# Hybrid RG-LRU / retention block on one core: gelus of the gate branch in groups, exponentials and roots in blocks, and the softplus spread over the convolution

## The chip, the cores and the metric

The kernel runs on one core of one Trainium2 chip. The metric is the device time of one execution in microseconds. TensorE (PE in the profile) multiplies matrices, VectorE (DVE) and ScalarE (ACT) do elementwise work, SyncE (SP) starts the loads. Each engine takes its instructions in a fixed order; an instruction waits until what it reads is written and until the buffer that it writes is free. ScalarE's functions live in tables: a function that is not in the table at hand needs an ACT_TABLE_LOAD ahead of it, which the compiler puts in.

## What is computed

A transformer-like block on 528 tokens (16 meta tokens and 512 of input), width 1024. One wide projection feeds a recurrent branch, a gate, a retention branch and two output gates; a feed-forward part follows. The change concerns the recurrent branch and its gate:

```python
u_rnn, u_gate, q, k, v, g_ret, ga, gb = jnp.split(rms_norm(h, norm_mix_g) @ w_in, IN_SPLITS, axis=-1)
xr = causal_dwconv(u_rnn, rnn_conv_w, rnn_conv_b)
# rg_lru, in 10 blocks of 128 channels:
r = sigmoid(xr @ w_a + b_a);  i = sigmoid(xr @ w_x + b_x)
log_a = -8.0 * r * softplus(-lam)
a = exp(log_a);  b = sqrt(-expm1(2.0 * log_a)) * (i * xr)
h_t = a_t * h_(t-1) + b_t
o_a = hr * gelu(u_gate)
```

`q` and `k` then get a rotary embedding, and retention follows.

## The kernel before

The tokens lie along the free axis (528 columns, the last 514 of them for the gate and for q), 128 channels on the partitions. Weights arrive as fp32 (`raw`, three buffers of 1 MB each) and are split into a high and a low fp16 half (`wt`, ten buffers): `split` (L94, L95) takes the high half on ScalarE and the low half on VectorE. Three fp16 products stand for one fp32 product, so a projection of 128 channels is 48 matmuls. A new weight load may start when VectorE has done the splits of the unit that held its buffer; `tick()` puts one split into the program at a time.

The stages around the change, in program order:

- Ten convolution steps. Step n multiplies u_rnn's block n (`conv_product`), from step 3 on multiplies the two gates of block n-3 (`rnn_gates`: two groups of six matmuls, two sigmoids on ScalarE, L663, one product on VectorE, L665), and applies the four taps (`conv_taps`: one ScalarE instruction L645, three VectorE instructions L647). `conv_split` splits the result (`xs`).
- The softplus of lambda on a 128 x 10 tile (L710 to L727): one absolute value, one exponential, 24 small VectorE instructions, a series for the logarithm.
- Ten gate products (loop at L732). Each takes 48 matmuls, one split, a gelu straight out of PSUM (L737), and by a table (`SPREAD`) groups of five of the recurrent branch's steps: tanh (`rnn_tanh`, L668), exponential with two VectorE products (`rnn_decay`, L672, L674, L675), square root (`rnn_root`, L678), and the scan over tokens (`rnn_scan`, a product L682 and a scan L683). The gates of blocks 7, 8 and 9 fall into the first three of them.
- For each of four heads the projections of q and k with their rotary embedding (`rotary`): two products, then on VectorE for each of two halves a product with the cosines (L773), one with the sines (L774) and their sum (L775), and a split. The second L773 and the second L774 are the last readers of the two PSUM tiles. Between them stand the remaining scans and the gating of the branch (`branch_a`, product L750 and a split). Products take PSUM tiles from a pool of four, so a projection needs a tile that the rotary of the projection before last still reads.

Until the tenth gate product the order on TensorE, ScalarE and VectorE is that of the program (`manual_schedule`, closed by `order.close()` at L754); behind it a scheduler orders the instructions. In retention, `head_norm` takes a square root (L1057) and the gate units copy PSUM with L892.

Of the kernel before, what the change touches and what calls it, by code (L numbers as in the profile page):

```python
# [21 lines left out]
NR = DR // P  # L22
# [4 lines left out]
TQ = T - T0  # L27
# [5 lines left out]
SW = 2.0 ** 8  # L33
S_XN = 4.0
# [19 lines left out]
def hybrid_block_kernel(ctx, tc, x, meta, norm_mix_g, w_in, conv_w, conv_b, rg_a_w, rg_a_b,  # L54
                        rg_x_w, rg_x_b, lam, w_brnn, w_bret, w_out, norm_ffn_g, w_up,
                        fconv_w, fconv_b, w_down, norm_final_g, rope_t, decay_t, out):
    nc = tc.nc
    const = ctx.enter_context(tc.tile_pool(name="const", bufs=1))
# [17 lines left out]
    def acc(name):  # L76
        return psum["acc"].tile([P, 2, 512], F32, name=name, tag="acc")
# [115 lines left out]
    def unit_load(cuts=1):  # L193

        nk, ncol, parts, fast = units[len(loaded)]
        raw = wraw.tile([P, 2048], F32, name="raw")
        n = nk * ncol
        rv = raw[:, :n].rearrange("p (k c) -> p k c", k=nk)
        for k0, c0, ap in parts:
            load(rv[:, k0:k0 + ap.shape[1], c0:c0 + ap.shape[2]], ap)  # L200
        loaded.append(len(loaded))
        if fast:
            return fast_steps(rv, nk // 2, ncol // 2)
        hk = nk // 2
# [12 lines left out]
        return [step(i, c) for i in range(2) for c in range(cuts)]
# [74 lines left out]
    ahead = [6]  # L292
    current = [0]

    def unit_tiles(u):
        return 4 if units[u][3] else 2

    def emit_step():
        u, run = steps[done[0]]
        while len(loaded) < min(u + 3, len(units)):  # L300
            queue(unit_load())
        run()
        done[0] += 1

    def queue(new):
        steps.extend((len(loaded) - 1, run) for run in new)
# [9 lines left out]
    def tick(n=1, late=True):  # L316


        for _ in range(n):
            if done[0] == len(steps):  # L320
                if len(loaded) == len(units):
                    return
                queue(unit_load())
            u = steps[done[0]][0]
            if sum(unit_tiles(i) for i in range(current[0], u + 1)) > ahead[0]:
                return
            if gating[0] and not late and hasattr(steps[done[0]][1], "late"):
                return
            emit_step()
# [10 lines left out]
    vt1 = const.tile([P, P], F32, name="vt1")  # L340
# [72 lines left out]
    def x_of(hi, lo):  # L413
        tv = (hi, lo)
        return lambda a, k, c0, n: tv[a][:, k, c0:c0 + n]
# [7 lines left out]
    def run_of(ps, halves, j=0, n=None):  # L423
        c0 = 512 - halves[0][1] + j
        n = n or halves[0][1] + halves[1][1]
        return ps.rearrange("p a b -> p (a b)")[:, c0:c0 + n]

    def project(ps, w, col, src, halves, nk, turns=False):

        both = [0, 1]  # L430
        for hfs in [both] if turns else [[0], [1]]:
            for k, (aw, ax), hf in [(k, s, hf) for k in range(nk) for s in SPLIT for hf in hfs]:
                    c0, n = halves[hf]
                    nc.tensor.matmul(half_of(ps, halves, hf), w(aw, k, col, P), src(ax, k, c0, n),  # L434
                                     start=k == 0 and (aw, ax) == (0, 0), stop=k == nk - 1 and aw == 1)
# [6 lines left out]
    HQ = [(XF + T0, 256), (XF + T0 + 256, 258)]  # L442
# [167 lines left out]
    half_r, half_t, half_x, gate_g = {}, {}, {}, {}  # L610

    def part(hv, n):
        if n not in hv:
            hv[n] = piece([P, T], F32, "rnn")
        return hv[n]
# [27 lines left out]
    def conv_taps(n, ps):  # L643
        xv = part(half_x, n)
        nc.scalar.activation(xv, run_of(ps, HR, 3, T), AF.Identity, scale=cwr[:, 30 + n:31 + n], bias=b_conv[:, n:n + 1])  # L645
        for j in (2, 1, 0):
            nc.vector.scalar_tensor_tensor(xv, run_of(ps, HR, j, T), cwr[:, 10 * j + n:10 * j + n + 1], xv,  # L647
                                           op0=ALU.mult, op1=ALU.add)
# [6 lines left out]
    def rnn_gates(n):  # L655
        xs = xr_split.pop(n)
        xr = part(half_x, n)
        gi = wtile("gi")
        for nm, bias, dst in (("a", b_a, part(half_r, n)), ("x", b_x, gi)):
            ps = acc("ps")  # L660
            wt = gw[nm][0][n // 4]
            project(ps, lambda a, k, c0, m: wt[:, a, n % 4 * P:n % 4 * P + P], 0, x_of(xs[:, 0], xs[:, 1]), HG, 1)
            nc.scalar.activation(dst, run_of(ps, HG), AF.Sigmoid,  # L663
                                 scale=1.0 / (SW * S_XR), bias=bias[:, n:n + 1])
        nc.vector.tensor_mul(xr, xr, gi)  # L665

    def rnn_tanh(n):
        nc.scalar.activation(part(half_t, n), part(half_r, n), AF.Tanh, scale=cpos[:, n:n + 1])  # L668
# [11 lines left out]
    def rnn_scan(n):  # L680
        r, t, xr = part(half_r, n), part(half_t, n), part(half_x, n)
        nc.vector.tensor_mul(t, t, xr)  # L682
        nc.vector.tensor_tensor_scan(xr, r, t, 0.0, op0=ALU.mult, op1=ALU.add)  # L683

    LAG = 3
    load_gates("a")
    load_gates("x")
    queue(unit_load())
    for n in range(NR):
        ps = conv_product(n)  # L690
        if n == 0:
            split_gates("a")
        if n >= LAG:
            tick(2 if n in (4, 6, 8) else 1)
            rnn_gates(n - LAG)
        conv_taps(n, ps)
        if n == 0:
            conv_split(0)
        if n == 1:
            split_gates("x")  # L700
        if n == 2:
            tick()
            conv_split(1)
            psum_layout(acc=4)
        if n >= 2:
            conv_split(n)


    lv = vt1[:, 70:80]
    sp = const.tile([P, 8, NR], F32, name="sp")  # L710
    nc.vector.tensor_scalar(sp[:, 0], lv, -1.0, 0.0, op0=ALU.mult, op1=ALU.max)
    nc.scalar.activation(sp[:, 1], lv, AF.Abs)
    nc.scalar.activation(sp[:, 2], sp[:, 1], AF.Exp, scale=-1.0)
    nc.vector.tensor_scalar_add(sp[:, 3], sp[:, 2], 2.0)
    nc.vector.reciprocal(sp[:, 4], sp[:, 3])
    nc.vector.tensor_mul(sp[:, 4], sp[:, 4], sp[:, 2])
    nc.vector.tensor_mul(sp[:, 5], sp[:, 4], sp[:, 4])
    nc.vector.memset(sp[:, 6], 1.0 / 15.0)
    for m in (13, 11, 9, 7, 5, 3, 1):
        nc.vector.tensor_mul(sp[:, 6], sp[:, 6], sp[:, 5])  # L720
        nc.vector.tensor_scalar_add(sp[:, 6], sp[:, 6], 1.0 / m)
    nc.vector.tensor_mul(sp[:, 6], sp[:, 6], sp[:, 4])
    nc.vector.scalar_tensor_tensor(sp[:, 7], sp[:, 6], 2.0, sp[:, 0], op0=ALU.mult, op1=ALU.add)
    cneg = const.tile([P, NR], F32, name="cneg")
    cpos = const.tile([P, NR], F32, name="cpos")
    nc.vector.tensor_scalar_mul(cneg, sp[:, 7], -8.0)
    nc.vector.tensor_scalar_mul(cpos, sp[:, 7], 8.0)  # L727


    ahead[0] = 6  # L730
    SPREAD = ((rnn_tanh, 2, 0), (rnn_decay, 3, 0), (rnn_tanh, 4, 5), (rnn_decay, 5, 5), (rnn_root, 7, 0), (rnn_scan, 7, 0), (rnn_root, 9, 5))
    for n in range(NR):  # L732
        ps = acc("ps")
        u, col = u_ug[n // 2], (n % 2) * P
        project(ps, get(u), col, xf, HQ, KD)
        tick()
        nc.scalar.activation(part(gate_g, n)[:, :TQ], run_of(ps, HQ),  # L737
                             AF.Gelu_apprx_tanh, scale=1.0 / (SW * S_XN))
        if n < LAG:
            rnn_gates(NR - LAG + n)  # L740
        for f, n0, m0 in SPREAD:
            if n == n0:
                for i in range(m0, m0 + 5):
                    f(i)

    oa = {}

# [30 lines left out]
            split(dst[m][:, 0, :n], dst[m][:, 1, :n], turned[m][:, :n], s)  # L778

    def between(i):  # L780
        if i < 5:
            rnn_scan(5 + i)
        for n in ((i,), (5, 6), (7, 8), (9,))[max(0, i - 4)]:
            branch_a(n)

# [442 lines left out]
    for i in range(2):  # L1228
# [5 lines left out]
        ps = branch(u_ba, oa_of, NR)  # L1234
# [311 lines left out]
    for j in range(12):  # L1546
# [21 lines left out]
        else:  # L1568
# [4 lines left out]
            for m in range(2):  # L1573
                f = 2 * j + m
# [210 lines left out]
```

## Time and profile before

| | |
|---|---|
| time, median of 3 runs | 1058.54 us (1058.52 to 1058.54) |
| the profiled execution | 1058.55 us |
| its span, first to last instruction | 1056.8 us |
| TensorE busy | 1038.8 us |
| VectorE busy | 872.0 us |
| ScalarE busy | 594.3 us |
| granted TensorE clock | 0.999 of full speed |

The convolution steps run to about 86 us of the span, the gate products from 81 to 138 us on TensorE, the rotary projections from 138 to 225.5 us. A row of the timeline has the start, the time until the group's last end, engine, line, operation, output and inputs, shapes, and how many instructions it merges; in brackets stands the engine's idle time before it and what ended that. Engines overlap neighbouring instructions a little, so a row's duration is somewhat longer than the distance to the next start. A row of groups has busy time, the mean of one in ns, and the idle time before them. A row of waits has who waited for whom, the total, how often, and the longest. In a row of stretches stand, behind the two bounds and the length, the busy times of PE, PEld (weight loads), DVE, ACT and POOL, then the granted clock, DMA's share and GB/s.

### The profile page before, as it was taken

To read this page: it belongs to the slowest core of one execution; us is meant where nothing else is said; L and a number is where in the kernel's file an instruction comes from. 1 tells how busy PE (TensorE), PEld (TensorE's weight loads), DVE (VectorE), ACT (ScalarE), POOL (GpSimd) and SP (SyncE) were. 2 spreads that over 40 slices of the span, in tenths; PEclk is the share of its full clock that TensorE was granted. 3 is DMA by queue.
4 is the path that set the end of the run, shared out by engine and by line. 5 is a ranking of instruction groups with operands and counts; after the bars stand their busy time and mean duration, and the time that the engine had idled before them with its cause. 6 is when DMAs were issued, how large, how long until landed. Compare 5 with 4: busy or idle time off the path is not lost.

```text
span 1056.8 us, 21446 instructions
## 1 busy us (share of the span) xinstructions
PE 1038.8 (98%) x9187; PEld 866.2 (82%) x9187; DVE 872.0 (83%) x1327; ACT 594.3 (56%) x942; POOL 6.9 (1%) x20
## 2 busy tenths in 40 slices
PE   8999999999999999999999999999999999999997
PEld 6888888875588888888888886588888888888884
DVE  6885799989669999997797785479989898988965
ACT  7558973444356758666454453375555555454432
POOL 2000000000000000000000000000000000000000
PEclk9999999999999999999999999999999999999999
DMA  9241253331013132334333355032433324114312
GB/s 295 94 132 58 81 180 120 123 120 41 1 41 113 49 106 74 102 111 154 102 115 120 111 209 180 1 120 81 160 102 99 120 81 144 58 61 145 96 41 80
DMA packets 109311, 111.52 MB, mean 106 GB/s; under 512 B 5674, under 2 KB 101136, under 8 KB 109216
## 3 DMA queue, kind: packets, MB, share of 16 engines
q1 hardware_dynamic: 108640, 109.74, 32.5%
q8 instruction: 72, 1.18, 0.5%
q10 hardware_dynamic: 288, 0.27, 0.1%
q0 software_dynamic: 288, 0.14, 0.1%
q14 instruction: 23, 0.19, 0.1%
HBM read 108.04 MB, written 2.10 MB: 104 GB/s over the span
## 4 chain that ended last, share of the span: by engine, by line
PE 74%; DVE 15%; ACT 8%; issue 2%; DMA 0%; ACTq 0%; DVEq 0%
PE ps L434 27%; PE P L1603 10%; PE pa L886 9%; DVE wt L95 4%; PE pe L886 4%; PE ps L1320 4%; PE pm L434 3%; PE ps L448 3%; PE pb L886 2%; PE ps L950 2%; PE pa L1490 2%; ACT wt L94 2%; PE ps L1040 2%; PE pa L974 1%; DVE raw L262 1%
## 5 line engine op out<-in xcount | busy, mean ns | idle before, releaser
L434 PEld LDWEIGHTS <-wt 128*128 128x128 f16 x3840 | 372.8, 97 | 53.4 <-issue 1.3
L95 DVE SCALAR_TENSOR_TENSOR wt<-raw,wt 128x1024 f16<-128x1024 f32 (+2 forms) x286 | 310.4, 1102 | 54.0 <-ACT wt L94 52.9
L94 ACT ACTIVATE wt<-raw 128x1024 f16<-128x1024 f32 (+2 forms) x286 | 267.8, 958 | 117.8 <-PE P L1603 23.1
L886 PEld LDWEIGHTS <-wt 128*128 128x128 f16 x2016 | 195.3, 97 | 32.4 <-issue 5.7
L434 PE MATMUL ps<-x2h,wt 128*128 128x258 f16 (+1 forms) x1184 | 196.2, 273 | 0.0
L434 PE MATMUL ps<-xh,wt 128*128 128x258 f16 (+4 forms) x1056 | 177.5, 275 | 1.6 <-DVE t L773 1.6
L434 PE MATMUL ps<-x2l,wt 128*128 128x256 f16 (+1 forms) x592 | 161.0, 272 | 0.0
L434 PE MATMUL ps<-xl,wt 128*128 128x256 f16 (+4 forms) x528 | 140.8, 274 | 0.0
L1603 PE MATMUL P<-wt,act 128*128 128x256 f16 x792 | 88.3, 273 | 0.0
L1603 PEld LDWEIGHTS <-act 128*128 128x128 f16 x792 | 77.4, 98 | 9.0
L886 PE MATMUL pa<-xs,wt 128*128 128x258 f16 x576 | 71.3, 273 | 1.9 <-ACT kept L892 1.5
L1468 DVE SCALAR_TENSOR_TENSOR cv<-ps,vt,cv 128x512 f32<-128x512 f32 x80 | 59.5, 747 | 9.1 <-ACT cv L1466 8.5
L434 PE MATMUL pm<-oa,wt 128*128 128x256 f16 (+1 forms) x480 | 54.1, 273 | 0.0
L262 DVE TENSOR_TENSOR raw<-raw 128x1024 f32<-128x1024 f32 x43 | 52.5, 1220 | 0.7
L886 PE MATMUL pa<-ob,wt 128*128 128x257 f16 x384 | 45.7, 274 | 0.6 <-ACT last L892 0.5
L1320 PE MATMUL ps<-wt,mx 128*128 128x512 f16 x192 | 44.3, 379 | 0.0
L950 PE MATMUL ps<-wt,xh 128*128 128x512 f16 x128 | 38.3, 379 | 0.7 <-ACT qk L94 0.5
L1466 ACT ACTIVATE cv<-ps,vt,vt 128x512 f32<-128x512 f32 x40 | 30.5, 766 | 11.9 <-PE ps L434 11.9
L1490 PEld LDWEIGHTS <-wt 128*128 128x128 f16 x336 | 32.6, 97 | 4.4
L1320 PEld LDWEIGHTS <-mx 128*128 128x128 f16 x192 | 17.6, 98 | 18.5
L94 ACT ACTIVATE qk<-t 128x514 f16<-128x514 f32 (+1 forms) x16 | 10.2, 638 | 39.6 <-DVE t L775 39.6
L448 PEld LDWEIGHTS <-wt 128*128 128x128 f16 x288 | 27.9, 97 | 5.0 <-issue 0.5
(327 smaller groups left out, 1504.5 us busy)
## 6 DMA issues: line engine op xcount, KB each, us to landing
raw<-in_w_in SPq DMA_DIRECT2D x36, 1024.0 KB, 5.1
raw<-in_w_up SPq DMA_DIRECT2D x24, 1024.0 KB, 5.2
raw<-in_w_down SPq DMA_DIRECT2D x48, 256.0 KB, 3.7
raw<-in_w_branch_ret SPq DMA_DIRECT2D x16, 512.0 KB, 4.9
raw<-in_w_in SPq DMA_DIRECT2D x12, 512.0 KB, 4.8
raw<-in_w_branch_rnn SPq DMA_DIRECT2D x8, 640.0 KB, 4.7
raw<-in_w_out SPq DMA_DIRECT2D x4, 1024.0 KB, 5.1
xin<-in_x SPq DMA_DIRECT2D x4, 512.0 KB, 5.8
```

The costliest lines, as they stand in the source:

```text
L94: a = nc.scalar.activation(hi, src, AF.Copy, scale=s)
L95: b = nc.vector.scalar_tensor_tensor(lo, src, s, hi, op0=ALU.mult, op1=ALU.subtract)
L262: nc.vector.tensor_tensor(pair, pair, rv[:, :, right].rearrange("p (h k) c -> p h k c", h=2), op=ALU.add)
L434: nc.tensor.matmul(half_of(ps, halves, hf), w(aw, k, col, P), src(ax, k, c0, n), start=k == 0 and (aw, ax) == (0, 0), stop=k == nk - 1 and ...
L448: mm = nc.tensor.matmul(half_of(ps, halves, hf), w(aw, k, col, P), src(ax, k, c0, n), start=k == 0 and (aw, ax) == (0, 0), stop=k == KD - ...
L886: nc.tensor.matmul(ps[:, :n], ws[k // 4](wf, aw, k % 4), src(xf_, ax, k), start=first and k == 0 and (aw, ax) == (0, 0), stop=k == last_k ...
L950: nc.tensor.matmul(pb, xf(ax, k, XF + j0, nb), w(aw, k % 4, 0, 512), start=i == 0, stop=i == 23)
L1320: nc.tensor.matmul(ps[:, n], mx[k][:, a, c0:c0 + P], wo[k // 2](aw, k % 2, n * 512, 512), start=k == 0 and (a, aw) == (0, 0), stop=k == ks ...
L1466: nc.scalar.activation(vv_, taps[2], AF.Identity, scale=vt2[:, 96 + ch:97 + ch], bias=bias)
L1468: nc.vector.scalar_tensor_tensor(vv_, taps[j], vt2[:, 48 * j + ch:48 * j + ch + 1], vv_, op0=ALU.mult, op1=ALU.add)
L1490: nc.tensor.matmul(ps[:, :258], w(wf, aw, k), x2_form(xf_, ax, k), start=first and k == 0 and (aw, ax) == (0, 0), stop=k == 3 and aw == 1, ...
L1603: nc.tensor.matmul(pd[:, 256 * tt:256 * tt + 256], t[:, ax, c0 + tt * P:c0 + tt * P + P], w(wf, aw, i), start=q % 6 == 0 and tt == 0 and i ...
```

## The change

The softplus is cut in two. `softplus_exp` puts its first maximum, the absolute value and the exponential into convolution step 2. `softplus_rest` is a generator that gives out the VectorE instructions in five pieces, in steps 3 to 7, ahead of the split of the step; the series is written with fewer instructions (a product and an addition in one, no memset), so 16 are left. The tanhs of blocks 0 to 5 move into steps 8 and 9, between the taps and the split.

In the gate loop, all products but those of 5, 8 and 9 are copied out of PSUM with the scale (AF.Copy), and their gelus are done later in place: 0 to 4 ahead of 5's, 6 and 7 ahead of 8's. A product's gelu or copy now comes behind the recurrent steps that two tables, FIRST and THEN, place in its turn. Exponentials are done in turns 2, 3 and 4, roots in turns 6 and 7, eight of the ten scans in turns 7 to 9. The gates of blocks 8 and 9 are both put behind product 1.

```diff
+    def softplus_exp():
+        lv = vt1[:, 70:80]
+        nc.vector.tensor_scalar(sp[:, 0], lv, -1.0, 0.0, op0=ALU.mult, op1=ALU.max)
+        nc.scalar.activation(sp[:, 1], lv, AF.Abs)
+        nc.scalar.activation(sp[:, 2], sp[:, 1], AF.Exp, scale=-1.0)
+
+    def softplus_rest():
+        nc.vector.tensor_scalar_add(sp[:, 3], sp[:, 2], 2.0)
+        nc.vector.reciprocal(sp[:, 4], sp[:, 3])
+        nc.vector.tensor_mul(sp[:, 4], sp[:, 4], sp[:, 2])
+        yield
...
         conv_taps(n, ps)
+        if LAG <= n < 8:
+            next(series)
+        if n >= 8:
+            for i in range(3 * (n - 8), 3 * (n - 8) + 3):
+                rnn_tanh(i)
...
         if n == 2:
+            softplus_exp()
             tick()
...
-    SPREAD = ((rnn_tanh, 2, 0), (rnn_decay, 3, 0), (rnn_tanh, 4, 5), (rnn_decay, 5, 5), (rnn_root, 7, 0), (rnn_scan, 7, 0), (rnn_root, 9, 5))
+    FIRST = {0: (rnn_tanh, (6,)), 1: (rnn_tanh, (7,)), 2: (rnn_tanh, (8, 9)), 5: ("gelu", range(5)), 6: (rnn_root, range(5)), 7: (rnn_root, range(5, 10)),
+             8: ("gelu", (6, 7))}
...
+    def gate_gelu(i, src=None, s=1.0):
+        g = part(gate_g, i)[:, :TQ]
+        nc.scalar.activation(g, g if src is None else src, AF.Gelu_apprx_tanh, scale=s)
...
-        nc.scalar.activation(part(gate_g, n)[:, :TQ], run_of(ps, HQ),
-                             AF.Gelu_apprx_tanh, scale=1.0 / (SW * S_XN))
-        if n < LAG:
-            rnn_gates(NR - LAG + n)
...
+        if n in (5, 8, 9):
+            gate_gelu(n, run_of(ps, HQ), 1.0 / (SW * S_XN))
+        else:
+            nc.scalar.activation(part(gate_g, n)[:, :TQ], run_of(ps, HQ), AF.Copy, scale=1.0 / (SW * S_XN))
+        for i in ((7,), (8, 9))[n] if n < 2 else ():
+            rnn_gates(i)
...
     def between(i):
-        if i < 5:
-            rnn_scan(5 + i)
+        if i < 2:
+            rnn_scan(8 + i)
```

On ScalarE, this stands from the gelu or copy of gate product 3 on, before (L737 gelus, L672 exponentials, L668 tanhs, L94 weight splits):

```order
L737 ACT_TABLE_LOAD
L737 ACTIVATE rnn<-ps 128x514
L672 ACT_TABLE_LOAD
L672 ACTIVATE rnn<-rnn,cneg 128x528 x5
L94 ACTIVATE wt<-raw 128x1024
L737 ACT_TABLE_LOAD
L737 ACTIVATE rnn<-ps 128x514
L668 ACTIVATE rnn<-rnn,cpos 128x528 x5
L94 ACTIVATE wt<-raw 128x1024
```

and from the copy of product 3 on now (L767 copies, L753 gelus, L678 roots):

```order
L767 ACTIVATE rnn<-ps 128x514
L94 ACTIVATE wt<-raw 128x1024
L672 ACTIVATE rnn<-rnn,cneg 128x528 x4
L767 ACTIVATE rnn<-ps 128x514
L94 ACTIVATE wt<-raw 128x1024
L753 ACT_TABLE_LOAD
L753 ACTIVATE rnn<-rnn 128x514 x5
L753 ACTIVATE rnn<-ps 128x514
L94 ACTIVATE wt<-raw 128x1024
L678 ACT_TABLE_LOAD
L678 ACTIVATE rnn<-rnn 128x528 x5
L767 ACTIVATE rnn<-ps 128x514
```

The table loads between gelus and exponentials are gone there, and one load serves six gelus.

On VectorE, this stands around the rotary of head 0's q before (the scans L683 are printed as SCALAR_TENSOR_TENSOR; `t` is the rotary's tile, L773 to L775 its steps):

```order
L773 TENSOR_TENSOR t_1956<-ps,rope_1842 128x514
L683 SCALAR_TENSOR_TENSOR rnn<-rnn 128x528
L95 SCALAR_TENSOR_TENSOR wt<-raw,wt 128x1024
L682 TENSOR_TENSOR rnn<-rnn 128x528 x2
L683 SCALAR_TENSOR_TENSOR rnn<-rnn 128x528
L95 SCALAR_TENSOR_TENSOR wt<-raw,wt 128x1024 x2
L774 TENSOR_TENSOR t_1957<-ps,rope_1843 128x514
L773 TENSOR_TENSOR t_1961<-ps,rope_1842 128x514
```

and now (the rotary's steps are L798 to L800, the branch products L775):

```order
L775 TENSOR_TENSOR rnn<-rnn 128x514
L95 SCALAR_TENSOR_TENSOR wt<-raw,wt 128x1024
L798 TENSOR_TENSOR t_1961<-ps,rope_1847 128x514
L95 SCALAR_TENSOR_TENSOR wt<-raw,wt 128x1024
L775 TENSOR_TENSOR rnn<-rnn 128x514 x5
L799 TENSOR_TENSOR t_1962<-ps,rope_1848 128x514
L798 TENSOR_TENSOR t_1966<-ps,rope_1847 128x514
```

All ten scans now stand ahead of the rotary, and seven of the ten branch products stand ahead of its second half. Before, seven scans and no more than three branch products did, and three scans and the other branch products stood between the later rotary steps.

On SyncE, one more load of 1 MB stands ahead of the two loads of the rotary's tables (`rope`), thirteen now where there were twelve. On ScalarE, the square root in `head_norm` of head 0 (L1057, now L1082) gets a table load of its own. Behind the rotary of the last head the instructions of TensorE and VectorE stand in the same order in both kernels.

More of the change, by code (lines that the diff above doesn't have):

```diff
@@ L683, in rnn_scan @@
         nc.vector.tensor_tensor_scan(xr, r, t, 0.0, op0=ALU.mult, op1=ALU.add)
+    cneg = const.tile([P, NR], F32, name="cneg")
+    cpos = const.tile([P, NR], F32, name="cpos")
+    sp = const.tile([P, 8, NR], F32, name="sp")
+    def softplus_exp():
[8 more added lines that the diff above has]
+        yield
+        nc.vector.tensor_mul(sp[:, 5], sp[:, 4], sp[:, 4])
+        nc.vector.tensor_scalar_mul(sp[:, 6], sp[:, 5], 1.0 / 15.0)
+        for m in (13, 11, 9, 7, 5, 3):
+            nc.vector.scalar_tensor_tensor(sp[:, 6], sp[:, 6], 1.0 / m, sp[:, 5], op0=ALU.add, op1=ALU.mult)
+            if m in (13, 7):
+                yield
+        nc.vector.scalar_tensor_tensor(sp[:, 6], sp[:, 6], 1.0, sp[:, 4], op0=ALU.add, op1=ALU.mult)
+        yield
+        nc.vector.scalar_tensor_tensor(sp[:, 7], sp[:, 6], 2.0, sp[:, 0], op0=ALU.mult, op1=ALU.add)
+        nc.vector.tensor_scalar_mul(cneg, sp[:, 7], -8.0)
+        nc.vector.tensor_scalar_mul(cpos, sp[:, 7], 8.0)
+        yield
+    series = softplus_rest()
     LAG = 3
@@ L706, in hybrid_block_kernel @@
             conv_split(n)
[L709 to L727, printed above, removed]
-    ahead[0] = 6
-    SPREAD = ((rnn_tanh, 2, 0), (rnn_decay, 3, 0), (rnn_tanh, 4, 5), (rnn_decay, 5, 5), (rnn_root, 7, 0), (rnn_scan, 7, 0), (rnn_root, 9, 5))
+    ahead[0] = 6
+    FIRST = {0: (rnn_tanh, (6,)), 1: (rnn_tanh, (7,)), 2: (rnn_tanh, (8, 9)), 5: ("gelu", range(5)), 6: (rnn_root, range(5)), 7: (rnn_root, range(5, 10)),
+             8: ("gelu", (6, 7))}
+    THEN = {2: (rnn_decay, (0, 1)), 3: (rnn_decay, range(2, 6)), 4: (rnn_decay, range(6, 10)),
+            7: (rnn_scan, range(3)), 8: (rnn_scan, (3, 4)), 9: (rnn_scan, range(5, 8))}
+    def gate_gelu(i, src=None, s=1.0):
+        g = part(gate_g, i)[:, :TQ]
+        nc.scalar.activation(g, g if src is None else src, AF.Gelu_apprx_tanh, scale=s)
     for n in range(NR):
@@ L736, in hybrid_block_kernel @@
         tick()
-        nc.scalar.activation(part(gate_g, n)[:, :TQ], run_of(ps, HQ),
-                             AF.Gelu_apprx_tanh, scale=1.0 / (SW * S_XN))
-        if n < LAG:
-            rnn_gates(NR - LAG + n)
[L741 to L744, printed above, removed]
+        for what in (FIRST, THEN):
+            f, ms = what.get(n, (None, ()))
+            for m in ms:
+                (gate_gelu if f == "gelu" else f)(m)
+        if n in (5, 8, 9):
[4 more added lines that the diff above has]
+            rnn_gates(i)
     oa = {}
```

## The prediction

> **What bounds the kernel now.** I read the page first, then TensorE's waits, then the stretches of time.
>
> ```profile
> PE 1038.8 (98%) x9187; PEld 866.2 (82%) x9187; DVE 872.0 (83%) x1327; ACT 594.3 (56%) x942; POOL 6.9 (1%) x20
> 60.00:150.00 90.00, 90.00 (x813) 78.75 (x811) 66.90 (x101) 75.58 (x99) 0.00 (x0) 1.00 0.29 95
> 184.00:221.00 37.00, 37.00 (x335) 32.21 (x333) 35.85 (x51) 16.44 (x23) 0.00 (x0) 1.00 0.38 118
> PE ps L434 <- DVE t L773: 1.6, 2, 1.0
> ```
>
> TensorE is the bound: 98% busy, and busy for all 90.00 us from 60 to 150, the very stretch in which the change sits (first number after the length). ScalarE's load there, 75.58 us, hides behind it. Nothing taken from ScalarE or VectorE shortens the kernel unless TensorE waits for it somewhere. The only such place near the change is the last row: two waits of matmuls (L434) for a rotary multiply (L773).
>
> ```profile
> 169.66 0.27 PE L434 MATMUL ps<-xl,wt 128*128 128x258 f16 x1
> 169.77 0.27 PE L434 MATMUL ps<-xh,wt 128*128 128x258 f16 x1
> 170.64 0.29 PE L434 MATMUL ps<-xh,wt 128*128 128x264 f16 x1 [0.60 <-DVE t L773]
> ...
> 181.39 0.28 PE L434 MATMUL ps<-xh,wt 128*128 128x264 f16 x1
> 182.67 0.27 PE L434 MATMUL ps<-xh,wt 128*128 128x256 f16 x1 [1.00 <-DVE t L773]
> ...
> 169.89 0.70 DVE L773 TENSOR_TENSOR t<-ps,rope 128x528 f32<-128x528 f32 x1
> ...
> 177.06 1.25 DVE L683 TENSOR_TENSOR_SCAN rnn<-rnn 128x528 f32<-128x528 f32 x1
> 178.23 3.09 DVE L750 TENSOR_TENSOR rnn<-rnn 128x514 f32<-128x514 f32 x5
> ...
> 181.84 0.68 DVE L773 TENSOR_TENSOR t<-ps,rope 128x514 f32<-128x514 f32 x1
> ```
>
> The products of k of head 1 and q of head 2 need a PSUM tile that the rotary of two projections earlier still reads; that rotary stands late in VectorE's queue, behind a scan and five branch products (from 177.06 to the end of the row at 178.23). Matmuls are issued 0.11 us apart (169.66 to 169.77), so the next was due at 169.88 and came at 170.64: 0.76 us lost. The second was due at 181.50 and came at 182.67: 1.17 us. Together **1.93 us**: all that this stage can give.
>
> **The change, part by part.** *Table loads.* The loads between 85 and 147 us, and one of them with its neighbours:
>
> ```profile
> L737 ACT ACT_TABLE_LOAD x7 | 9.0, 1283 | 0.1
> L663 ACT ACT_TABLE_LOAD x3 | 3.8, 1283 | 0.1
> L672 ACT ACT_TABLE_LOAD x2 | 2.6, 1283 | 0.0
> L678 ACT ACT_TABLE_LOAD x2 | 2.6, 1283 | 0.0
> ...
> 87.23 1.04 ACT L94 ACTIVATE wt<-raw 128x1024 f16<-128x1024 f32 x1
> 88.29 1.28 ACT L737 ACT_TABLE_LOAD   x1
> 89.58 0.60 ACT L737 ACTIVATE rnn<-ps 128x514 f32<-128x514 f32 x1
> ```
>
> These 14 and the softplus's own one make 15; four remain in the stage. That frees 11 x 1.3 = 14 us of ScalarE; seven more passes over a gate tile (0.6 us each, a copy and a later gelu in place of one gelu) take back 4 us. On the path: nothing, TensorE was not waiting for them. The trace prices a switch at 1.3 us: the split ends at 88.27, the gelu starts at 89.58. The Trainium skill (ScalarE: Activation LUTs, What ACT_TABLE_LOAD costs) has a drain of about 1.38 us beside the load, 2.66 us for each switch, and by it 11 loads would free 29 us; the trace agrees on the load (1283 ns) and shows no gap for the drain. Whether more is hidden in a switch is weighed under rival 1.
>
> *Softplus.* It leaves 86.4 to 91.7 and its small operations go, two or three at a time, into five convolution steps.
>
> ```profile
> 86.36 0.17 DVE L711 TENSOR_SCALAR sp<-vt 128x10 f32<-128x10 f32 x1
> ...
> 91.61 0.17 DVE L727 TENSOR_SCALAR cpos<-sp 128x10 f32<-128x10 f32 x1
> DVE xs L95 <- ACT xs L94: 3.6, 5, 0.8
> ACT xs L94 <- DVE rnn L647: 12.4, 5, 2.5
> 39.18 0.64 ACT L94 ACTIVATE xs<-rnn 128x528 f16<-128x528 f32 x1 [2.76 <-DVE rnn L647]
> ```
>
> Three cost about 0.6 us (0.2 apart) and stand where VectorE waits 0.7 us for ScalarE's high half anyway. The early exponential with its load (1.7 us) falls into the 2.76 us idle before 39.18, and three tanhs each in steps 8 and 9 (0.6 apiece, like the gelus below) into the 2.5 us idle of a step. Price 0; were that cover gone, at most some 0.1 us a step, on engines that TensorE does not wait for there.
>
> *The new place of ScalarE's and VectorE's work.* This decides. From product 2 on TensorE goes at the same pace in both kernels: five gate products lie between the first two rows, so 5.29 us each.
>
> ```profile
> 111.56 0.27 PE L434 MATMUL ps<-xl,wt 128*128 128x256 f16 x1
> 138.00 0.27 PE L434 MATMUL ps<-xl,wt 128*128 128x256 f16 x1
> 159.42 0.27 PE L434 MATMUL ps<-xl,wt 128*128 128x256 f16 x1
> ...
> 131.80 2.78 ACT L678 ACTIVATE rnn<-rnn 128x528 f32<-128x528 f32 x5
> L1044 ACT ACTIVATE or<-ps 128x514 f32<-128x514 f32 x16 | 9.5, 593 | 7.6 <-PE ps L1040 7.6
> L1482 ACT ACTIVATE cv<-cv 128x512 f32<-128x512 f32 x24 | 15.1, 627 | 28.3 <-DVE cv L1468 28.3
> ...
> 144.74 3.47 DVE L95 SCALAR_TENSOR_TENSOR wt<-raw,wt 128x1024 f16<-128x1024 f32 x3
> 135.93 1.25 DVE L683 TENSOR_TENSOR_SCAN rnn<-rnn 128x528 f32<-128x528 f32 x1
> 137.10 0.69 DVE L682 TENSOR_TENSOR rnn<-rnn 128x528 f32<-128x528 f32 x1
> ```
>
> Product 4 is ready at about 111.7 and ScalarE, now ahead, waits for it. Then in its new order: copy to 112.3, split to 113.25, load to 114.55, six gelus (0.53 apart) and a split to 118.75, load to 120.05, five roots to 122.85, copy of product 6 (ready 122.3) and the eighth split of the stage, to 124.3. VectorE, idle before, does the low half of that split until 125.4 and then has everything that stands ahead of the second L798 (L773 before) of head 0's q: ten products L682 (0.61: 6.1), ten scans (1.17, from 135.93 to 137.10: 11.7), seven branch products (0.60, from 178.23: 4.2), eight splits (1.13: 9.0) and three rotary steps (1.8). That is 32.8, to 158.2, and 0.1 for the last one's tail: **158.3**. TensorE needs the tile at 159.3 (159.42 is the second matmul of that product). Margin 1.0. Next, k of head 0: 10.7 us of queue further, 169.0 against 169.88: margin 0.9. q of head 1: 7.8 further, 176.8 against 180.74: margin 3.9, where before there was a wait, because the block of five at 178.23 is done by then. So both waits go: -1.93 us, and nothing is late next until 229.5:
>
> ```profile
> 214.67 1.23 DVE L95 SCALAR_TENSOR_TENSOR wt<-raw,wt 128x1024 f16<-128x1024 f32 x1 [0.96 <-ACT wt L94]
> ...
> 229.53 0.39 PE L950 MATMUL ps<-wt,xh 128*128 128x512 f16 x1 [0.46 <-ACT qk L94]
> ```
>
> VectorE had caught up ahead of that in before too (it stands idle before 214.67), so this wait is paced by TensorE and should shift along with everything else, unchanged.
>
> *Moved beside it.* The gates of block 9 go ahead of product 2; product 2 then needs, at 95.7 (three products ahead of 111.56), the tile of block 8's first gate. ScalarE waits for product 1 there, ready at 93.1, and then has a copy and that sigmoid to do, some 1.4 us: 94.5, cost 0, margin 1.2. The two rope loads now stand on SyncE's queue behind one more weight load, which waits for a split of VectorE; and head 0's first root needs a table load, since the last table is now the gelu's.
>
> ```profile
> 133.34 1.05 SPq L758 DMA_DIRECT2D rope<-rope  x2
> rope<-rope SPq DMA_DIRECT2D x2, 264.0 KB, 5.4
> 294.33 0.39 ACT L892 ACTIVATE kept<-pa 128x257 f32<-128x257 f32 x1 [0.32 <-PE pa L886]
> 296.04 0.69 ACT L1057 ACTIVATE rt<-ps,eps_t 128x514 f32<-128x514 f32 x1 [1.32 <-PE ps L1055]
> ```
>
> The weight load's two splits end at about 140.7, so the ropes issue near 141 to 142 and land 5.4 later, by 148; the first rotary step comes at 152.3. Cost 0, cover 4 us. The added table load (1.28) fits the 1.32 us in which ScalarE waits before 296.04: 0; uncovered it would cost at most 1.3.
>
> **Sum.** The profiled execution took 1058.55 us (span 1056.8, 1.75 around it; the median is 1058.54, the same to 0.01). 1058.55 - 1.93 = **1056.6 us**. Bounds: 0 gained if each wait comes back in another place; 2.5 if the lost time at 229.5 (0.6 by the issue spacing) goes too.
>
> **The rivals.** (1) *The wait moves to head 0.* My margins of 1.0 and 0.9 rest on a queue of 30-odd rows; 2% of it is 0.7. If VectorE is late by x beyond 1.0, q of head 1 waits x and the gain shrinks to 1.93 - x: between 1056.6 and 1058.5, about 1057.6. For it: the margins. Against: each duration is a row's, and the start at 125.4 hangs on TensorE's own pace. One such case: a switch that holds ScalarE for as long again as its load, unseen here. Two loads stand between product 4 and the eighth split, so 2 x 1.28 = 2.6 late, 1.6 lost, 1058.2; the start at 89.58 speaks against it, 0.02. The switch of 2.66 us that the Trainium skill gives (same page and section) would be this case. Chance of (1) in all 0.12.
>
> (2) *Slower: the ropes land late.* If the weight load ahead of them keeps its old place in time, 147.15, instead of moving forward, the ropes land at 153.6 by the 5.4 us, or at some 156 if the load before slows them. The first rotary step, and all behind it on VectorE, then starts up to 3.8 late, 2.8 beyond the margin: 1059.5. It decides from a landing at 153.3; at 155.2 the change has lost what it gains. Against it: the splits that free the buffer come earlier by the sum above. Chance 0.06.
>
> (3) *More goes.* The wait at 229.5 follows a weight load that VectorE's backlog may have delayed: then 1056.0. Against: VectorE was already waiting there in before. Chance 0.12.
>
> (4) *Nothing arrives.* The stage ends 1.9 earlier, but a wait downstream takes it back, for instance the new table load in head 0's norm: 1058.5. Against: behind the rotary the instructions of TensorE and VectorE stand in the same order as before, and they wait for one another rather than for fixed times. Chance 0.08.
>
> **How the numbers follow.** The forecast has 0.62. The range takes in the forecast, (1), (3) and most of (4): 1056.0 to 1058.5, which leaves out (2) and the edges. About 0.2%, 2.1 us, is what a measurement can tell here; the forecast lies just inside it. Faster: (3) and the edge of the forecast, 0.20. Slower by over 0.2%, beyond 1060.7: half of (2), 0.03. Same: 0.77.
>
> **What would show it.** Right: no wait of L434 for a rotary multiply, ScalarE with four table loads between 85 and 147 us and idle times ended by TensorE there, the eighth split of the stage at 123 to 124, head 0's second L798 ending near 158.3, the wait at 229.5 still there some 1.9 earlier. Wrong: a wait for L798 at q of head 1 (rival 1), VectorE idle until a rope lands (2), the same 1.9 missing at 184 but back by 300 (4), or TensorE idle inside the gate products, for which I have no price.

## The result, and the profile after

The changed kernel takes **1056.72 us** (median; 1056.47 to 1057.10) where the kernel before, beside it, takes 1058.58 us (1058.42 to 1058.98): ratio 0.9982, 95% interval [0.9976, 0.9989], 1.86 us less. Forecast: 1056.6. The profiled execution has a span of 1054.8 us against 1056.8. TensorE's line and its waits from 150 us on (the columns of a wait: us in all, times, longest):

```profile
PE 1039.1 (99%) x9187; PEld 866.4 (82%) x9187; DVE 870.8 (83%) x1319; ACT 587.2 (56%) x940; POOL 6.9 (1%) x20
...
PE ps L975 <- ACT qk L94: 0.5, 1, 0.5
```

The row of L434 waiting for the rotary multiply is gone; the other rows are within 0.1 us of what they were. TensorE's rows at the three places that the prediction names are now ordinary rows without a bracket:

```profile
159.15 0.27 PE L434 MATMUL ps<-xl,wt 128*128 128x256 f16 x1
...
169.73 0.28 PE L434 MATMUL ps<-xl,wt 128*128 128x264 f16 x1
...
180.57 0.27 PE L434 MATMUL ps<-xl,wt 128*128 128x256 f16 x1
...
227.33 0.39 PE L975 MATMUL ps<-wt,xh 128*128 128x512 f16 x1 [0.45 <-ACT qk L94]
```

The last row is the wait of 229.53, 2.20 earlier. Of that, 1.93 is the two waits; 0.27 is a difference between the two profiled runs at their start (TensorE's first products with the input begin at 6.48 us here and at 6.76 before, ahead of anything that the change touches). So 0.27 is to be added to a time of this trace before it is held against the forecast.

VectorE, and the two stretches as the prediction showed them:

```profile
123.95 1.23 DVE L95 SCALAR_TENSOR_TENSOR wt<-raw,wt 128x1024 f16<-128x1024 f32 x1 [4.30 <-ACT wt L94]
125.09 0.70 DVE L682 TENSOR_TENSOR rnn<-rnn 128x528 f32<-128x528 f32 x1
...
157.41 0.68 DVE L798 TENSOR_TENSOR t<-ps,rope 128x514 f32<-128x514 f32 x1
...
168.07 0.70 DVE L798 TENSOR_TENSOR t<-ps,rope 128x528 f32<-128x528 f32 x1
...
175.85 0.68 DVE L798 TENSOR_TENSOR t<-ps,rope 128x514 f32<-128x514 f32 x1
...
60.00:150.00 90.00, 90.00 (x812) 78.73 (x811) 71.36 (x90) 66.39 (x94) 0.00 (x0) 1.00 0.35 112
184.00:221.00 37.00, 37.00 (x334) 32.18 (x332) 30.70 (x44) 14.59 (x20) 0.00 (x0) 1.00 0.34 109
```

The eighth split is done at 125.18, the three products that free a tile end at 158.09, 168.77 and 176.53. VectorE (third busy figure of a stretch, behind TensorE and its weight loads) does 71.36 us of work from 60 to 150 where it did 66.90, and has 30.70 left from 184 to 221 where it had 35.85: some five microseconds of work came forward. In the kernel before, VectorE's work without a pause begins here:

```profile
123.73 0.71 DVE L674 TENSOR_TENSOR a<-rnn 128x528 f32<-128x528 f32 x1 [1.30 <-ACT rnn L672]
```

So that work begins at nearly the same time in both kernels. Before, it began with the ten products behind the second five exponentials (L674 and L675, until 130.55), and the first product of a scan (L682) stood at 132.82. Now the exponentials come earlier on ScalarE, those products are done by 116.5, and the scans begin at 125.09. ScalarE has its four loads in the stage (one is shown), and idle times that end with TensorE:

```profile
111.39 0.60 ACT L767 ACTIVATE rnn<-ps 128x514 f32<-128x514 f32 x1 [1.24 <-PE ps L434]
111.88 1.05 ACT L94 ACTIVATE wt<-raw 128x1024 f16<-128x1024 f32 x1
112.95 1.28 ACT L753 ACT_TABLE_LOAD   x1
114.24 2.72 ACT L753 ACTIVATE rnn<-rnn 128x514 f32<-128x514 f32 x5
...
292.54 1.28 ACT L1082 ACT_TABLE_LOAD   x1
293.84 0.69 ACT L1082 ACTIVATE rt<-ps,eps_t 128x514 f32<-128x514 f32 x1
296.04 0.39 ACT L917 ACTIVATE kept<-pa 128x257 f32<-128x257 f32 x1 [1.51 <-PE pa L911]
```

The added load of head 0's norm (292.54) is hidden: the root behind it starts at 293.84, which is 2.20 earlier than the 296.04 of before, as TensorE's rows are, and the copy behind that still waits 1.51 us for TensorE.

### The profile page after: what moved, and what is told of

It is laid out like the page before. It is cut to its first block, busy times and chain, and to the rows that moved or that the text cites. A ratio compares the mean times of both kernels' runs of the same rounds, so it can differ in the third digit from the quotient of the medians.

```text
span 1054.8 us, 21439 instructions
## 1 busy us (share of the span) xinstructions
PE 1039.1 (99%) x9187; PEld 866.4 (82%) x9187; DVE 870.8 (83%) x1319; ACT 587.2 (56%) x940; POOL 6.9 (1%) x20
## 4 chain that ended last, share of the span: by engine, by line
PE 84%; DVE 11%; ACT 3%; issue 1%; DMA 0%; ACTq 0%; DVEq 0%
PE ps L434 36%; PE P L1628 10%; PE pa L911 9%; PE pe L911 4%; PE ps L1345 4%; PE pm L434 3%; DVE wt L95 3%; PE ps L448 3%; PE pb L911 2%; PE ps L975 2%; PE pa L1515 2%; PE ps L1065 2%; PE pa L999 1%; ACT wt L94 1%; DVE raw L262 1%
## 5 line engine op out<-in xcount | busy, mean ns | idle before, releaser
L434 PEld LDWEIGHTS <-wt 128*128 128x128 f16 x3840 | 372.8, 97 | 51.4
L94 ACT ACTIVATE wt<-raw 128x1024 f16<-128x1024 f32 (+2 forms) x286 | 268.1, 959 | 127.7 <-PE P L1628 23.1
L434 PE MATMUL ps<-x2h,wt 128*128 128x258 f16 (+1 forms) x1184 | 196.2, 272 | 0.0
L434 PE MATMUL ps<-xh,wt 128*128 128x258 f16 (+4 forms) x1056 | 177.0, 274 | 0.0
L434 PE MATMUL ps<-x2l,wt 128*128 128x256 f16 (+1 forms) x592 | 160.9, 272 | 0.0
L434 PE MATMUL ps<-xl,wt 128*128 128x256 f16 (+4 forms) x528 | 140.7, 274 | 0.0
L434 PE MATMUL pm<-oa,wt 128*128 128x256 f16 (+1 forms) x480 | 54.1, 273 | 0.0
L1065 PE MATMUL ps<-sc,v 128*128 128x257 f16 (+4 forms) x384 | 31.7, 236 | 0.0
```

The lines of the kernel that those rows point to most:

```text
L94: a = nc.scalar.activation(hi, src, AF.Copy, scale=s)
L1065: nc.tensor.matmul(ps[:, hf, s0 - lo_i:257], vd, st[SCP[b][0]][:, sa, o:o + hi_i - s0], start=i == 0, stop=i == len(todo) - 1)
```

## The experiments

Theory: the whole gain is the 1.93 us that TensorE waited for a PSUM tile at the rotary, and it comes because VectorE starts its queue of scans and branch products earlier; a tile that comes free late costs its lateness less a margin of about 0.9 us. Rivals: the freed table loads are themselves the gain; the softplus spread is; the new place of the scans is. Each kernel was timed beside the kernel before (1058.56 to 1058.67 us). Medians of 11 runs, ratios to before:

| kernel | us | range | ratio [95%] |
|---|---|---|---|
| changed, tile freed 1 product later | 1056.94 | 1056.70–1057.22 | 0.9984 [0.9975, 0.9993] |
| changed, tile freed 3 products later | 1058.22 | 1058.04–1058.34 | 0.9995 [0.9986, 1.0004] |
| changed + 4 table loads | 1056.77 | 1056.66–1057.01 | 0.9984 [0.9974, 0.9993] |
| changed, gelus one by one | 1060.51 | 1060.35–1061.01 | 1.0019 [1.0010, 1.0028] |
| changed, scans written as before | 1056.66 | 1056.54–1057.06 | 0.9982 [0.9973, 0.9991] |
| changed, softplus in one lump | 1056.72 | 1056.53–1056.87 | 0.9982 [0.9973, 0.9991] |
| before + softplus spread | 1057.79 | 1057.70–1058.02 | 0.9993 [0.9984, 1.0002] |
| before, scans and branch products held back | 1058.52 | 1058.20–1059.00 | 0.9999 [0.9990, 1.0008] |
| before, held back, 5 branch products left out | 1056.63 | 1056.53–1056.97 | 0.9979 [0.9970, 0.9988] |
| before, held back (nothing left out), next block held too | 1057.11 | 1056.91–1057.75 | 0.9986 [0.9978, 0.9995] |
| changed, next block held back | 1056.39 | 1056.20–1056.67 | 0.9979 [0.9970, 0.9988] |

The intervals are some 2 us wide, so differences of less than 1 us between these kernels rest on the ranges and on the traces, not on the intervals.

**Is lateness the price?** The product that frees the tile is done twice, or four times, in the rotary of head 0's queries:

```diff
-            nc.vector.tensor_mul(t1[:, :n], run_of(pp[m], halves), cs)
+            for _ in range(1 + again * m):
+                nc.vector.tensor_mul(t1[:, :n], run_of(pp[m], halves), cs)
...
-        rotary(u_q[h], t[0], HQ, TQ, T0, S_QK / (SW * S_XN))
+        rotary(u_q[h], t[0], HQ, TQ, T0, S_QK / (SW * S_XN), 1 if h == 0 else 0)
```

> The changed kernel with VectorE's product that frees the accumulator for head 1 (the second product with the cosines, queries of head 0) done twice: its end moves from 158.1 to 159.3 us, as a subtraction moves ahead of it too, and TensorE needs the accumulator at 159.04. The result is the same. Theory (cost = lateness less the margin of 0.95 us): a wait of 0.25 us, 1057.0 us (1056.7 to 1057.2). Rival (VectorE's time is charged as such): 0.6 to 1.2 us, 1057.3 to 1057.9. Rival (several accumulators cover it): 1056.7 us and no wait.

Measured 1056.94, 0.22 above the changed kernel: as the theory has it, not the 0.6 to 1.2 of the added work. Its trace, VectorE and then TensorE (the loop adds a line to the kernel, so the rotary's products are L799 and L800 here, and their sum L801):

```profile
158.82 0.68 DVE L799 TENSOR_TENSOR t<-ps,rope 128x514 f32<-128x514 f32 x1
```

```profile
158.82 0.39 PE L434 MATMUL ps<-xh,wt 128*128 128x264 f16 x2
159.05 0.28 PE L434 MATMUL ps<-xl,wt 128*128 128x264 f16 x1
159.16 0.68 PE L434 MATMUL ps<-xh,wt 128*128 128x264 f16 x2
```

The product ends at 159.50. Two matmuls in a row take 0.39 elsewhere; the pair at 159.16 takes 0.68, so 0.29 us is lost there, though no bracket says so. With three more products (`3 if h == 0`):

> The changed kernel with the same product done four times: the accumulator comes free at 161.7 us instead of 158.1. The result is the same. Theory: TensorE waits from 159.04 to 161.7, 2.65 us, and no more at the keys, whose need shifts along: 1059.3 us (1059.0 to 1059.6), slower than the kernel before. Rival (VectorE's time is charged as such): three products, 1.8 us, 1058.5 us. Rival (several accumulators cover it): 1056.7 us.

Measured 1058.22: 1.50 more, where the theory had 2.65. Nearest is the rival that charges VectorE's time as such, with 1.8; but one product more cost 0.2 and not 0.6, and the trace has two waits for tiles that make the sum. TensorE and its waits:

```profile
159.32 0.28 PE L434 MATMUL ps<-xh,wt 128*128 128x264 f16 x1
160.33 0.28 PE L434 MATMUL ps<-xh,wt 128*128 128x256 f16 x1 [0.73 <-DVE t L800]
...
286.89 5.35 PE L1066 MATMUL ps<-sc,v 128*128 128x257 f16 x65 [0.56 <-DVE sf L853]
PE ps L1066 <- DVE sf L853: 0.6, 1, 0.6
```

```profile
159.59 0.68 DVE L800 TENSOR_TENSOR t<-ps,rope 128x514 f32<-128x514 f32 x1
160.19 0.68 DVE L799 TENSOR_TENSOR t<-ps,rope 128x514 f32<-128x514 f32 x1
```

I had the wrong tile. The releaser is L800 (ends 160.27), the last reader of the *other* of the two tiles; this is now the one that is free first, and the product starts as soon as it is. Due at 159.43, come at 160.33: 0.90 lost. The tile with the repeated products is free at 162.08; the next product takes a tile some 5.3 us behind this one, and no wait shows there. A second wait of 0.6 is new at 286.89, in head 0's value products, where the changed kernel has none; 0.90 and 0.6 make the 1.50. That the second comes from the tiles having swapped places 127 us earlier fits the trace, in which the engines' order is the same there, but was not tested by itself.

**Are the table loads the price?** Tiny square roots and a gelu force four more loads:

```diff
+        if n == 1:
+            nc.scalar.activation(sq_t, eps_t, AF.Sqrt)
...
+    nc.scalar.activation(sq_t, eps_t, AF.Sqrt)
+    nc.scalar.activation(sq_t, eps_t, AF.Gelu_apprx_tanh)
```

> The changed kernel with four table loads more (5.1 us of ScalarE): two ahead of gate copy 1, where ScalarE waits 2.58 us for TensorE, and two behind the last gelu, where it waits 7.2 us for weights; the order of VectorE, TensorE and the load queue is untouched. Theory: loads cost nothing where ScalarE waits; block 8's first sigmoid comes 0.2 to 0.3 us later against a margin of 1.2: 1056.7 us (1056.5 to 1057.0). Rival (freed loads themselves are the gain): 2 to 5 us more, 1058.7 to 1061.8 us.

Measured 1056.77, 0.05 above the changed kernel, which is less than the runs of one kernel differ: 5.1 us of loads cost next to nothing. ScalarE at the first place:

```profile
90.55 1.28 ACT L765 ACT_TABLE_LOAD   x1
91.84 0.20 ACT L765 ACTIVATE sq_t<-eps_t 128x1 f32<-128x1 f32 x1
93.13 0.60 ACT L769 ACTIVATE rnn<-ps 128x514 f32<-128x514 f32 x1 [1.08 <-PE ps L434]
93.75 1.28 ACT L663 ACT_TABLE_LOAD   x1
95.04 0.70 ACT L663 ACTIVATE rnn<-ps,vt 128x528 f32<-128x528 f32 x1
```

One detail of the expectation failed: the second load did not go in front of the copy but behind it (the copy needs none), so block 8's sigmoid is not 0.3 but 1.2 us late (95.04 against 93.50, less the 0.30 by which this run's copy is later). That is all of its margin: TensorE starts product 2 at 95.80 where the changed kernel has 95.33, which less the 0.30 is 0.17 lost, though no bracket says so.

**Gelus one by one.**

```diff
-    FIRST = {...  2: (rnn_tanh, (8, 9)), 5: ("gelu", range(5)), 6: (rnn_root, range(5)), 7: (rnn_root, range(5, 10)),
-             8: ("gelu", (6, 7))}
+    FIRST = {...  2: (rnn_tanh, (8, 9)), 6: (rnn_root, range(5)), 7: (rnn_root, range(5, 10))}
...
-        if n in (5, 8, 9):
+        if True:
             gate_gelu(n, run_of(ps, HQ), 1.0 / (SW * S_XN))
```

> The changed kernel with each gelu back in its own turn, straight from the accumulator: 10 table loads more, 7 passes fewer, about 9 us more of ScalarE between 87 and 135 us; the softplus stays spread and the roots stay together. Theory: by the durations of the trace the sigmoid of gate block 8 comes 2.4 us later against a margin of 1.2, so TensorE waits 1.1 us there; the eighth weight cut and the last roots come 3.9 to 5.2 us later, of which 1.1 is TensorE's own shift and 0.9 is margin, so 1.9 us more is waited at the rotary: 1059.7 us (1057.8 to 1060.5). Rival (each table load is paid): 9 us more, 1065 us. Rival (the spread softplus and the early roots are all there is): 1056.7 us.

Measured 1060.51: slower than before, 3.8 above the changed kernel, far from the 9 of the added ScalarE time, but 0.8 above the 1059.7 expected. TensorE waits at just the places named:

```profile
95.59 0.84 PE L434 MATMUL ps<-xs,gw 128*128 128x264 f16 x6 [0.24 <-ACT rnn L752]
97.60 0.27 PE L434 MATMUL ps<-xh,wt 128*128 128x256 f16 x1 [1.18 <-ACT rnn L663]
...
162.53 0.28 PE L434 MATMUL ps<-xh,wt 128*128 128x256 f16 x1 [1.05 <-DVE t L797]
...
173.89 0.29 PE L434 MATMUL ps<-xh,wt 128*128 128x264 f16 x1 [0.61 <-DVE t L797]
```

A matmul lasts 0.28 us here but the next is issued 0.11 behind it, so each wait loses 0.17 more than its bracket says: 0.4, 1.3, 1.2 and 0.8, together 3.7. The two at the rotary are the 1.9 expected (2.0); those at the gates are 1.7 instead of 1.1, since the gelu of turn 1 also holds a tile too long. Had the change not grouped the gelus, its other parts would have lost time. The earlier tanhs and the earlier roots were not undone by themselves, so their shares are not known.

**The place of the scans, the lump of the softplus.** The scans written as they were, with the roots still early:

```diff
-            7: (rnn_scan, range(3)), 8: (rnn_scan, (3, 4)), 9: (rnn_scan, range(5, 8))}
+            7: (rnn_scan, range(5))}
...
-        if i < 2:
-            rnn_scan(8 + i)
+        if i < 5:
+            rnn_scan(5 + i)
```

> The changed kernel with the scans written where they stood before: five in turn 7 and five between the rotary steps. In the order that results, all ten scans stand ahead of the last rotary products of head 0, since the roots are ready by 127 us. Theory: VectorE's queue starts as early as in the changed kernel and holds the same work, so the rotary is no later: 1056.7 us (1056.5 to 1057.1). Rival (where the scans are written is what brings the gain): 1058.5 us, with the wait of the head-0 keys back.

Measured 1056.66: the changed kernel's time. And the softplus in one lump, early:

```diff
-        if LAG <= n < 8:
-            next(series)
+        if n == 7:
+            softplus_exp()
+            for _ in series:
+                pass
...
         if n == 2:
-            softplus_exp()
```

> The changed kernel with the whole softplus in one lump in convolution step 7 instead of over five steps; one table load more, about 3 us of ScalarE and 16 short operations of VectorE in one step. Theory: the step has 2.8 us of waiting on ScalarE and 0.7 on VectorE, and three steps lie between a convolution step and the gates that need it, so what is late is taken up: 1056.7 us (1056.5 to 1057.2). Rival (spreading as such is the gain, because a lump stalls the convolution): 1058 us or more, with a wait of TensorE near 80 us.

Measured 1056.72. Neither the place of the scans in the text nor the spreading as such counts. In the order that results all ten scans still stand ahead of the last rotary products of head 0, so another place in the order itself is not tested here.

**The softplus alone**, moved out of the gate stage of the kernel before:

```diff
         conv_taps(n, ps)
+        if LAG <= n < 8:
+            next(series)
...
         if n == 2:
+            softplus_exp()
...
-    nc.scalar.activation(sp[:, 1], lv, AF.Abs)
-    nc.scalar.activation(sp[:, 2], sp[:, 1], AF.Exp, scale=-1.0)
...
```

> The kernel before with one part of the change: the softplus chain alone is spread over the convolution steps; gelus, tanhs, roots and scans stay where they were. Theory (the time goes where VectorE's queue starts later than TensorE's need of the rotary's accumulator): in the kernel before ScalarE has no idle time from 85 to 146 us, so taking Abs, one table load and the exponential (1.7 us) out of it at 85.6 us moves the whole chain up to the last roots and with it VectorE's scans and rotary by up to 1.7 us; of the two waits that sum to 1.93 us some 0.2 is left: 1056.9 us (1056.7 to 1057.6). Rival (the grouping of the gelus and the 11 table loads fewer are what counts): 1058.3 to 1058.6 us. Rival (only the place of the scans counts): 1058.5 us as well.

Measured 1057.79: 0.77 gained, not the 1.7 expected and not the 0 of the rivals. ScalarE at two places, then VectorE and TensorE at the rotary:

```profile
88.09 0.60 ACT L749 ACTIVATE rnn<-ps 128x514 f32<-128x514 f32 x1
...
99.87 0.60 ACT L749 ACTIVATE rnn<-ps 128x514 f32<-128x514 f32 x1 [0.86 <-PE ps L434]
```

```profile
157.39 0.68 DVE L785 TENSOR_TENSOR t<-ps,rope 128x514 f32<-128x514 f32 x1
```

```profile
180.75 0.28 PE L434 MATMUL ps<-xh,wt 128*128 128x264 f16 x1
182.03 0.27 PE L434 MATMUL ps<-xh,wt 128*128 128x256 f16 x1 [1.00 <-DVE t L785]
```

The first gelu starts 1.49 earlier than before (89.58), but gelu 2 then waits 0.86 us for its product, and 0.64 is left (99.87 against 100.51); VectorE has the same: 157.39 against 158.03. This profiled run began 0.14 later than the one before (TensorE's first products with the input at 6.90 against 6.76), so the lead is 0.8. It covers the first wait of 0.76, which is the time gained, and the second stands as it was: TensorE and VectorE are both earlier by the same. So the two waits are one debt of 1.93 us, paid in two parts, and an earlier start takes off it what arrives at VectorE.

**Is it the start or the order?** The kernel before with none of the change, and VectorE's scans and branch products held behind the product that frees the tile:

```diff
+    freed = [None]
     def between(i):
-        if i < 5:
-            rnn_scan(5 + i)
...
+        with tc.issue_after(freed[0]):
+            if i < 5:
+                rnn_scan(5 + i)
```

(`freed[0]` is set to the last `tensor_mul` with `cs`; the branch products stand in the same block.)

> The kernel before with nothing of the change: its table loads, its gelus and its softplus in one lump all stay. Only VectorE's order behind the gate stage is another: the scan and the branch products that are written behind a rotary step may not be taken ahead of that step's product that frees the accumulator. Theory (the whole gain is the 1.93 us that TensorE waits for that product): both waits go and the time is that of the changed kernel, 1056.7 us (1056.4 to 1057.0), though ScalarE has all 15 table loads. Rival (freed ScalarE time, or the spread softplus, brings part of the gain by itself): 1057.3 us or more. Rival (the scans held back are then late in the stage of the values): 1058 us or more, with new waits behind 230 us.

Measured 1058.52: nothing gained, and the theory as I had stated it falls. Both waits at the rotary are gone, and these came in their place:

```profile
PE ps L823 <- DVE t L773: 0.7, 1, 0.7
PE ps L953 <- ACT qk L94: 0.7, 1, 0.7
PE ps L823 <- DVE v L95: 0.3, 1, 0.3
PE ps L953 <- DVE v L95: 0.3, 1, 0.3
...
184.00:221.00 37.00, 37.00 (x334) 32.19 (x332) 37.00 (x54) 15.19 (x22) 0.00 (x0) 1.00 0.35 116
221.00:230.00 9.00, 7.63 (x61) 5.45 (x60) 8.97 (x14) 2.86 (x5) 0.00 (x0) 1.00 0.49 173
```

TensorE starts the first scores 1.89 us earlier than before (223.61, not 225.50), but VectorE is now busy for all 37.00 us from 184 to 221 and for 8.97 of the next 9, and the last head's rotary is late instead. From there to 303 us it loses 1.2 us more than the kernel before. Another 0.3 goes at 616. (The profiled execution, 1058.24, is one of the fastest of the eleven; 0.4 of the 1.93 is left in it, 0.1 by the medians.) This is the last rival of the expectation, though the waits come at 227 to 229 and not behind 230. The theory that took its place: the 1.93 us is a debt of VectorE, whatever the order in which it works it off. But this order has a price of its own, in VectorE's rows:

```profile
151.47 2.36 DVE L95 SCALAR_TENSOR_TENSOR wt<-raw,wt 128x1024 f16<-128x1024 f32 x2 [1.66 <-ACT wt L94]
154.56 1.22 DVE L95 SCALAR_TENSOR_TENSOR wt<-raw,wt 128x1024 f16<-128x1024 f32 x1 [0.73 <-ACT wt L94]
```

With the scans held back, VectorE stands idle for 2.4 us, waiting for the high halves of weights, where in the kernel before it worked on. That is more than the 1.2 us lost later. The same kernel with 3.0 us of VectorE's work left out:

```diff
-        nc.vector.tensor_mul(g, g, half_x.pop(n)[:, T0:])
+        hx = half_x.pop(n)[:, T0:]
+        if n < 5:
+            nc.vector.tensor_mul(g, g, hx)
```

> The kernel with the held-back scans once more, and five of the ten branch products (gelu times scan, the last five) left out, so that VectorE has 3.0 us less to do between 200 and 230 us; the output of the recurrent branch is not the reference's. What the first held-back run gave: no wait at the rotary, but 1.1 us more of waits at 227 to 229, and a time like before. Theory (the 1.93 us is a debt of VectorE, and holding work back only moves it to the next due time): with 3.0 us less to do the debt is paid before 227, no wait but the old one of 0.46 us is left there, 1056.7 us (1056.4 to 1057.0), all table loads kept. Rival (what is late at 227 is the held-back scans' roots or ScalarE, not VectorE's backlog): the waits at 227 to 229 stay, 1058.2 us or more.

Measured 1056.63, with ScalarE's 15 loads all there. TensorE waits from 60 to 260 us:

```profile
PE ps L955 <- ACT qk L94: 0.5, 1, 0.5
PE ps L825 <- DVE krep L814: 0.2, 1, 0.2
PE ps L955 <- DVE v L95: 0.2, 1, 0.2
```

These are the changed kernel's waits, and its time. So the debt is VectorE's, due first at the rotary and then, in the held-back order, at the last head; work done earlier, or not at all, pays it. That nothing else does is not shown: an order that frees the tile sooner and leaves VectorE no idle time was not run.

**The wait that is left**, 0.45 us at 227.33, follows a step of the next weight block that stands ahead of the last rotary products and waits 1.8 us for ScalarE. It is held behind them:

```diff
-        run()
+        hold = turned_q[0] and getattr(run, 'first', False)
+        with tc.issue_after(turned_q[0]) if hold else nullcontext():
+            run()
...
-            nc.vector.tensor_mul(t2[:, :n], run_of(pp[1 - m], halves), sn)
+            turned_q[0] = nc.vector.tensor_mul(t2[:, :n], run_of(pp[1 - m], halves), sn).ins
```

(`first` marks the step that cuts a fast weight block's top left quarter.) On the changed kernel:

> The changed kernel with VectorE's first step of the next weight block (a cut of 512 columns that waits 1.8 us for ScalarE at 222.9 us, and the sums behind it, 1.2 us) held behind the last rotary products of the last head. Theory: the wait of 0.45 us that is left at 227.3 us goes, since the rotary products can start as TensorE ends theirs at 223.5 and end by about 226.1: 1056.2 us (1056.0 to 1056.4). Rival (the block held back is then late itself, as a wait of the next products for the weights): 1056.7 us or more.

Measured 1056.39, 0.33 less than the changed kernel (the intervals of the ratios overlap). The wait is gone and a wait for values grew from 0.2 to 0.3:

```profile
PE ps L980 <- DVE v L95: 0.3, 1, 0.3
PE ps L850 <- DVE v L95: 0.2, 1, 0.2
```

It has the lowest median of the kernels that were run. On the kernel before with the work held back:

> The kernel before with the held-back scans and branch products and, besides, with the next weight block's first step held behind the last rotary products of the last head; nothing of the change. Theory: the wait of 0.46 us at 229.5 goes too, of which 0.1 is given back at the value products, as in the changed kernel with the same edit: 1056.35 us (1056.1 to 1056.7). Rival (the step held back is late now that VectorE has scans left to do there): 1056.7 us or more.

Measured 1057.11: 1.4 less than the held-back kernel without this edit, and 0.7 above the changed kernel with it. The trace has a wait for the copy `krep`, which stands in VectorE's backlog behind a branch product:

```profile
PE ps L828 <- DVE krep L817: 0.7, 1, 0.7
```

The time is that of the rival, but what is late is this copy and not the step held back. The profiled execution, at 1057.75, is as slow as the slowest of the eleven, 0.6 above their median, so this trace does not tell how much of the 0.7 between the medians this wait makes.

## Why the prediction was right

The forecast case came in; 1056.6 was 0.1 from the time. By its own steps:

- *What can be gained is 1.93 us of two waits.* Shown: both waits are absent, TensorE is 1.93 earlier behind them, and the kernel before with less work on VectorE takes 1056.63.
- *The ledger of VectorE's queue.* With 0.27 added, the trace has 125.45 for the eighth split (forecast 125.4), 158.36, 169.04 and 176.80 for the three products (158.3, 169.0, 176.8).
- *Margins of 1.0 and 0.9.* They are real and as thin as stated: the first is 0.95 in the trace (158.09 against 159.04), 1.2 us more cost 0.2 to 0.3, and the waits came back when the gelus were not grouped. Rival 1 was that near. Its form with a long switch fell: the load at 112.95 is followed by a gelu at 114.24, 1.29 later, and four loads added cost 0.05. The Trainium skill (ScalarE: Activation LUTs, What ACT_TABLE_LOAD costs) has 2.66 us for a switch; no run here shows more than the load, and in all of them the instruction behind a load starts 1.29 to 1.30 us after the load's start unless it waits for its input.
- *Table loads cost nothing on the path.* Shown by the added loads, to 0.17 us in the trace and 0.05 in the medians. But the sentence is true only while they stand in idle time: ten of them put back at other places cost 3.8 us through tiles freed late.
- *Softplus, price 0.* Shown with the lump. That moving it out of the gate stage is worth something by itself (0.77 in the kernel before) was not said: it gives ScalarE, and through it VectorE, a lead of 0.8 us.
- *Block 8's gate, margin 1.2.* Shown from both sides: 1.2 late cost 0.17; 2.8 late (96.85 against 93.50, less 0.54 by which that run began later) cost 1.7, of which 0.4 is the gelu of turn 1.
- *Ropes (rival 2).* They issue at 140.99 and land 5.4 later, ahead of the first rotary product at 152.05. (The sum of this rival gives 1059.4 and not 1059.5: 1056.6 and 2.8.)
- *The wait at 229.5 is paced by TensorE and stays.* It stayed, so rival 3 did not come. The reason given was too short: VectorE's order there makes it, and one step put back takes it away.
- *Rival 4.* Nothing downstream took it back: of the 2.20 at 227 us, 2.15 is still there at the last products.

What the prediction did not see is that the rotary's place in VectorE's queue is not enough: the one order tried without an earlier start brought nothing, since VectorE stood idle in it and was late at the last head. What counts is how much work is left at each due time.

## What to carry to other kernels

Where one engine is busy throughout, price a change to the others only at the places where it waits: list what its next buffer waits for, add up the queue ahead of that, and hold the end against the need. A wait that goes when work is put in another order may be a debt that falls due elsewhere: look whether the late engine has idle time between there and the next wait, and whether the new order gives it new idle time, before counting the gain. Time freed on a third engine (14 us of ScalarE's loads in the gate stage here; over the whole execution, with the added copies and two loads elsewhere, ScalarE is busy 7.1 us less) is worth what of it arrives as an earlier start of the late one.

## What the runs showed of the hardware that was not expected

A copy on ScalarE needed no table load of its own: in the run with added loads it ran at 93.13 behind a square root's load, and the load for the sigmoid came only behind it, at 93.75. The Trainium skill (ScalarE: Activation LUTs, Table sets: the hidden batching unit) has copy in every set, and the trace agrees. And a delay of one tile can cost less than it is: the tile freed 3.6 us late cost 0.9 at once and, it seems, 0.6 some 127 us later, which was not tested by itself.
